# A two-layer MLP in a streaming encoder: seven products in the second layer too, with input sums made in the first

## The chip, the core and the metric

The kernel runs on one NeuronCore of one Trainium2 chip. The metric is the device time of one execution in microseconds. Five engines work side by side, each through its own list of instructions in a fixed order: TensorE (PE, with its weight loads shown as PEld), VectorE (DVE), ScalarE (ACT), GpSimd (POOL) and SyncE (SP), which here issues all DMAs. Semaphores join them.

## The reference

One layer of a hybrid encoder: a token mixer and then an MLP with squared ReLU, on 512 tokens of width 2048 with a hidden width of 8192. All arithmetic is in float32. What matters here is the second sub-layer:

```python
h = x * (1.0 + sc2) + sh2
ff = jnp.square(jax.nn.relu(h @ w_ff1[l])) @ w_ff2[l]
x = layer_norm(ALPHA * x + g2 * ff, ln2_g[l], ln2_b[l])
```

`sc2`, `sh2` and `g2` come from `c @ w_ada + b_ada`, a product of one row with six matrices of 2048 x 2048. `x` is the output of the first sub-layer, `layer_norm(ALPHA * x + g1 * mix)`. `h @ w_ff1` and the product with `w_ff2` are 512 x 2048 x 8192 each.

## The kernel before, in words

A float32 operand is cut into a rounded high part and the rest (`split`, L114: ScalarE writes the high part by L57, VectorE the rest by L60), and every product is made as three matmuls: high x high, high x low, low x high (`mm3`, `mm3s`, `mm3n`, L188 to L204). Weights come from DRAM in loads of 1 MB into four buffers named `raw` (`load`, L118), and their splits go into three buffers each of `wh` and `wl`.

The order of each engine's instructions is set when the program is built: a scheduler takes what is ready in its own model of time, first by place in the program less an offset that `PRIO` (L25) gives to named groups. On the chip that order is fixed; an instruction that waits holds all those behind it on its engine.

*First MLP layer.* `acts` holds the layer's input, transposed and split. The hidden width is done in 16 units of 512. Unit 0 is a plain product. Units 1 to 15 (`ff1_unit`, L1086) use Winograd's form of Strassen's scheme: weights and input are each seen as 2 x 2 blocks, and seven products of half-sized blocks replace eight. The sums of the input (`t3`, `n2`, `n1`, `t4`, L1054 to L1084) are made once. The sums of the weights are made in each unit: eight additions on VectorE. A product is 48 matmuls of 256 columns in two halves of the inner dimension (`c`), each with a split of 128 x 1024. PSUM keeps three running banks: they are read out between accumulations, since some partial sums are used twice. The order of products is a11, s3, s2, a12, s1, a22, s4, and the second one needs three sums of weights. Each quarter of the result (two blocks of 128 features x 256 tokens) goes through ReLU and square on ScalarE and is stored to `h_d` in DRAM (L1145).

*Second MLP layer.* The 8192 hidden features are done in 8 parts of 1024 (`for e in range(NE)`). `hidden` (L1181) loads a part from `h_d` and splits it. `ff2` (L1214) does a block of 512 output features for it: two weight loads, 8 steps of 128 features, 4 token tiles, three matmuls of 512 columns, so 96 a block and 384 a part, in four banks. `ff2_done` (L1193) adds the banks to `ffa` on VectorE (part 0: ScalarE copies).

*Background work.* `bg` holds generators, and `tick` advances the first by one step. `w_quads` (L165) advances it by `pump[0]` steps per weight load. In the second layer these are two `ada_block` jobs, 8 steps each, that make the gate row `g2`; a step loads 1 MB and does two accumulations of 128 x 1024 on VectorE (L63). `pump[0]` is 1, so they lie in parts 0 and 1. Ahead of part 3 (`EB`) the sum so far is multiplied with `g2`, and `ALPHA` times the normalised residual, read back from `xn_d`, is added: 16 tiles of 128 x 512, four VectorE operations each. From part 3 on each bank takes two operations (multiply by `g2`, add).

The last part ends tile by tile with the layer norm statistics and the output.

Of the kernel before, what the change touches and what calls it, by code (L numbers as in the profile page):

```python
# [25 lines left out]
            wo=5000, ln1=150, ff1=3000, ff2=4000, tx=2000, ln2=150, index=-100, topk=60, rope=600, ssm0=600, ssm=300, glu=150,  # L26
# [25 lines left out]
def trunk_kernel(ctx, tc, A, out):  # L52
    nc = tc.nc
# [21 lines left out]
    pools = {n: ctx.enter_context(tc.tile_pool(name="ps_" + n, bufs=b, space=PSUM))  # L75
# [9 lines left out]
    def bank(n="mm"):  # L85
        return pools[n].tile([128, 512], F32, name=n)

# [888 lines left out]
    h_d = dram.tile([16, 128, 4, SEQ], F32, name="h_d")  # L976
# [66 lines left out]
    with prio("ff1"):  # L1043
        for m in range(4):
            r = ev_tile()
            act(r, banks[m], AF.Relu)
            act(r, r, AF.Square)
            nc.sync.dma_start(h_d[0][:, m], r)
# [37 lines left out]
    def ff1_unit(b):  # L1086
        lo, hi, s1, s2 = [None] * 2, [None] * 2, [None] * 2, [None] * 2
# [6 lines left out]
        ca, cb = slice(0, 256), slice(256, 512)  # L1094

        def form(name, c):
            a11, a21, a12, a22 = lo[c][:, :, ca], lo[c][:, :, cb], hi[c][:, :, ca], hi[c][:, :, cb]
            if name == "a11":
                return a11
            if name == "s3":  # L1100
                s1[c], s2[c] = st_tile(), st_tile()
                tt(s1[c], a21, a22, OP.add)
                tt(s2[c], s1[c], a11, OP.add)
                tt(a11, a11, a21, OP.add)
                return a11
            if name == "s2":
                return s2[c]
            if name == "a12":
                return a12
            if name == "s1":  # L1110
                return s1[c]
            if name == "a22":
                return a22
            tt(s2[c], s2[c], a12, OP.add)
            return s2[c]

        def product(ps, name, x, start, stop):
            for c in range(2):
                h = stage.tile([128, 4, 256], F32R, name="wh", bufs=3)
                l = stage.tile([128, 4, 256], F32R, name="wl", bufs=3)  # L1120
                with prio("w_split"):
                    split(h, l, form(name, c))
                for k in range(4):
                    for m in range(2):
                        w = slice(m * 128, m * 128 + 128)
                        mm3s(ps[:, m * 256:m * 256 + 256], h[:, k, w], l[:, k, w], x[:, 4 * c + k, 0],
                            x[:, 4 * c + k, 1], start and (c, k, m) == (0, 0, 0), stop and (c, k, m) == (1, 3, 1))

        def copy(ps):
            o = ev_tile()  # L1130
            with prio("ff1"):
                act(o, ps)
            return o

        def done(o, ps, m0, j, neg):

            with prio("ff1"):
                if o is None:
                    o = ev_tile()
                    act(o, ps, AF.Relu)  # L1140
                else:
                    tt(o, ps, o, OP.add)
                    act(o, o, AF.Relu, scale=-1.0 if neg else 1.0)
                act(o, o, AF.Square)
                nc.sync.dma_start(h_d[b][:, m0:m0 + 2, (lo_t, hi_t)[j]], o.rearrange("p (m n) -> p m n", m=2))  # L1145

        x, z, v = bank(), bank(), bank("sa")
        product(x, "a11", b11, True, False)
        e1 = copy(x)
        product(z, "s3", t3, True, False)  # L1150
        e3 = copy(z)
        product(x, "s2", n2, False, False)
        e2 = copy(x)
        product(v, "a12", b21, True, True)
        done(e1, v, 0, 0, False)
        product(x, "s1", n1, False, False)
        done(e3, x, 2, 1, True)
        product(z, "a22", t4, False, True)
        done(e2, z, 2, 0, True)
        product(x, "s4", b22, False, True)  # L1160
        done(None, x, 0, 1, False)

    for b in range(1, 16):
        ff1_unit(b)
    ph1.close()
    actp.close()

# [3 lines left out]
    NE, EB = 8, 3  # L1171
    HX = ctx.enter_context(tc.tile_pool(name="hx", bufs=1, reuse_waits="tile"))
    FF = ctx.enter_context(tc.tile_pool(name="ff", bufs=1, reuse_waits="tile"))
    ffa = FF.tile([128, NT, D], F32, name="ffa")
    g2 = FF.tile([128, D], F32, name="g2")
    AZ[0] = FF
    bg.extend(ada_block(6 + j, to_rows(lambda i, j=j: g2[:, (2 * j + i) * 512:(2 * j + i + 1) * 512]), True)
              for j in range(2))
    pump[0] = 1

    def hidden(e):  # L1181

        out = []
        for i in range(2):
            r = load(h_d[2 * e + i], [128, 4, 512])
            o = (TX if e == 0 else HX).tile([128, 4, 2, SEQ], F32R, name="tx", bufs=3)
# [4 lines left out]
        return out  # L1191

    def ff2_done(e, nb, t, ps):  # L1193
        cs_ = slice(nb * 512, (nb + 1) * 512)
        with prio("ff2"):
            o = ffa[:, t, cs_]
            if e == 0:
                act(o, ps)
            elif e < EB:
                tt(o, ps, o, OP.add)  # L1200
            else:
# [3 lines left out]
                if e == NE - 1:  # L1205
                    V.bn_stats(out=stats[:, t, nb], in_=o)
# [7 lines left out]
    def ff2(e, nb, h1):  # L1214
        banks = banks4()
# [6 lines left out]
    for e in range(NE):  # L1222
        h1 = hidden(e)
        if e == EB:
            while bg:
                tick()

            for nb in range(4):
                cs_ = slice(nb * 512, (nb + 1) * 512)
                g_ = FF.tile([128, 512], F32, name="lng")  # L1230
                b_ = FF.tile([128, 512], F32, name="lnb")
                nc.sync.dma_start(g_, A["ln1g"][0:1, cs_].to_broadcast([128, 512]))
                nc.sync.dma_start(b_, A["ln1b"][0:1, cs_].to_broadcast([128, 512]))
                ts(g_, g_, ALPHA, None, OP.mult)
                ts(b_, b_, ALPHA, None, OP.mult)
                for t in range(NT):
                    y = FF.tile([128, 512], F32, name="y", bufs=2)
                    nc.sync.dma_start(y, xn_d[t][:, cs_])
                    tt(y, y, g_, OP.mult)
                    tt(y, y, b_, OP.add)  # L1240
                    o = ffa[:, t, cs_]
                    tt(o, o, g2[:, cs_], OP.mult)
                    tt(o, o, y, OP.add)
        if e < NE - 1:
            for nb in range(4):
                ff2(e, nb, h1)
        if e == 0:
            txp.close()
# [118 lines left out]
```

## Time and profile before

| | |
|---|---|
| median of 3 runs | 2313.34 us (2308.38 to 2313.43) |
| the profiled execution | 2313.1 us |
| its span, first to last instruction | 2311.3 us |
| mean granted TensorE clock | 0.988 |
| read from HBM, written | 351.46 MB, 37.75 MB |

A window row of the profile gives a stretch of the span, its length, then for each engine the busy time and, in brackets, the number of instructions that were recorded (some matmuls are missing from a trace), then the granted TensorE clock, the DMA engines' busy share and GB/s. A timeline row gives start, duration, engine, source line, operation, output and inputs, and in brackets the idle time before it with what ended it. A group row gives source line, engine, operation, output and inputs, shape and count; then total busy time and the mean in ns; then the engine's idle time before such instructions and what ended it. Lines such as L57 and L60 are helpers, so groups are told apart by their tiles: `wh` and `wl` are split weights, `raw` a loaded one, `st` a sum of weights, `ev` a piece of hidden output, `adaz` the accumulator of a gate row.

### The profile page before, as it was taken

How to read it: one execution, taken by the hardware profiler on the slowest of the kernel's cores; microseconds unless marked ns; L12 is line 12 of the kernel's file. 1: busy time of each engine (PE TensorE's matmuls, PEld its weight loads, DVE VectorE, ACT ScalarE, POOL GpSimd, SP SyncE). 2: the span in 40 equal slices, each digit the busy share in tenths (PEclk: the TensorE clock that was granted, in tenths of full speed). 3: DMA queues.
4: the chain of work that ended last, by engine and by line, in shares of the span. 5: the costliest groups of instructions: out<-in, count | busy, mean ns of one | idle time of the engine just before them, and what ended most of it. 6: DMA issues, size and time to landing. Idle time of an engine off the chain costs nothing.

```text
span 2311.3 us, 30437 instructions
## 1 busy us (share of the span) xinstructions
PE 2224.7 (96%) x12283; PEld 1910.5 (83%) x12283; DVE 1636.8 (71%) x2300; ACT 967.1 (42%) x1400; POOL 15.7 (1%) x31
## 2 busy tenths in 40 slices
PE   6999999998889999989999999999999999999997
PEld 5778887766667888889999999999888888888886
DVE  7896899998766876676777677676454865545567
ACT  3323434547865214545555555554322222222232
POOL 0000000000000000000000000000000000000000
PEclk9999999999999999999999999999999999999999
DMA  8877562354233776733333333345664543233341
GB/s 313 314 303 266 181 237 92 125 192 144 82 107 111 293 287 233 239 128 108 139 119 142 133 138 137 117 147 206 224 218 146 171 157 128 110 123 133 110 146 73
DMA packets 114053, 391.18 MB, mean 169 GB/s; under 512 B 13428, under 2 KB 49652, under 8 KB 77176
## 3 DMA queue, kind: packets, MB, share of 16 engines
q1 hardware_dynamic: 113912, 389.24, 46.7%
q8 instruction: 96, 1.57, 0.3%
q14 instruction: 45, 0.37, 0.0%
HBM read 351.46 MB, written 37.75 MB: 168 GB/s over the span
## 4 chain that ended last, share of the span: by engine, by line
PE 80%; DVE 12%; ACT 4%; DMA 2%; issue 2%; SPq 0%; DVEq 0%; ACTq 0%
PE mm L202 9%; PE mm L204 9%; PE mm L203 9%; PE mm L197 7%; PE mm L196 7%; PE mm L198 7%; PE mm L191 4%; PE mm L192 4%; PE mm L190 4%; PE sa L204 2%; PE sa L202 2%; PE sa L203 2%; DVE wl L60 2%; ACT uc L57 2%; PE sa L197 1%
## 5 line engine op out<-in xcount | busy, mean ns | idle before, releaser
L57 ACT ACTIVATE wh<-raw 128x1024 fp32r<-128x1024 f32 x302 | 319.6, 1059 | 740.3 <-PE mm L204 519.7
L60 DVE TENSOR_TENSOR wl<-raw,wh 128x1024 fp32r<-128x1024 f32 x302 | 368.5, 1221 | 281.7 <-ACT wh L57 281.0
L63 DVE SCALAR_TENSOR_TENSOR adaz<-raw,cols,adaz 128x1024 f32<-128x1024 f32 (+2 forms) x212 | 239.4, 1138 | 26.3 <-DMA raw<-in_adaR_dram 20.0
L202 PE MATMUL mm<-wh,tx 128*128 128x512 f32 x600 | 234.6, 391 | 1.4 <-DVE ffa L60 1.4
L204 PE MATMUL mm<-wh,tx 128*128 128x512 f32 x600 | 234.1, 390 | 0.0
L203 PE MATMUL mm<-wl,tx 128*128 128x512 f32 x600 | 234.1, 390 | 0.0
L190 PE MATMUL mm<-acts,wh 128*128 128x512 f32 (+1 forms) x568 | 222.9, 396 | 7.2 <-ACT ve L57 3.8
L191 PE MATMUL mm<-acts,wl 128*128 128x512 f32 (+1 forms) x568 | 225.4, 397 | 1.2 <-DVE wl L60 0.9
L192 PE MATMUL mm<-acts,wh 128*128 128x512 f32 (+1 forms) x568 | 223.0, 393 | 0.0
L196 PE MATMUL mm<-tx,wh 128*128 128x256 f32 x720 | 203.5, 283 | 6.1 <-ACT wh L57 6.1
L197 PE MATMUL mm<-tx,wl 128*128 128x256 f32 x720 | 205.3, 285 | 0.9 <-DVE wl L60 0.9
L198 PE MATMUL mm<-tx,wh 128*128 128x256 f32 x720 | 204.6, 284 | 0.0
L197 PE MATMUL mm<-acts,wl 128*128 128x256 f32 x720 | 203.7, 283 | 0.0
L198 PE MATMUL mm<-acts,wh 128*128 128x256 f32 x720 | 203.7, 283 | 0.0
L196 PE MATMUL mm<-acts,wh 128*128 128x256 f32 x720 | 203.7, 283 | 0.0
L203 PE MATMUL mm<-wl,acts 128*128 128x512 f32 x448 | 175.2, 391 | 1.2 <-DVE wl L60 1.0
L204 PE MATMUL mm<-wh,acts 128*128 128x512 f32 x448 | 174.9, 391 | 0.0
L202 PE MATMUL mm<-wh,acts 128*128 128x512 f32 x448 | 174.2, 392 | 0.3 <-DVE z_t L60 0.2
L60 DVE TENSOR_TENSOR wl<-st,wh 128x1024 fp32r<-128x1024 f32 x90 | 110.2, 1225 | 88.9 <-ACT wh L57 88.9
L57 ACT ACTIVATE wh<-st 128x1024 fp32r<-128x1024 f32 x90 | 95.2, 1059 | 126.0 <-PE mm L198 107.4
L196 PEld LDWEIGHTS mm<-tx,wh 128*128 128x128 f32 x720 | 138.3, 192 | 6.7 <-ACT wh L57 6.7
L196 PEld LDWEIGHTS mm<-acts,wh 128*128 128x128 f32 x720 | 138.2, 192 | 0.0
(314 smaller groups left out, 4632.2 us busy)
## 6 DMA issues: line engine op xcount, KB each, us to landing
raw<-in_wff_dram SPq DMA_DIRECT2D x113, 1024.0 KB, 5.0
raw<-in_adaR_dram SPq DMA_DIRECT2D x64, 1024.0 KB, 4.9
raw<-in_adaS_dram SPq DMA_DIRECT2D x32, 1024.0 KB, 9.3
raw<-in_wo_dram SPq DMA_DIRECT2D x16, 1024.0 KB, 6.8
h_d<-ev SPq DMA_DIRECT2D x64, 256.0 KB, 3.8
raw<-h_d SPq DMA_DIRECT2D x16, 1024.0 KB, 4.8
rawx<-in_wff_dram SPq DMA_DIRECT2D x15, 1024.0 KB, 5.4
raw<-in_wconv_dram SPq DMA_DIRECT2D x12, 1024.0 KB, 5.5
```

Source lines behind the costliest of these rows:

```text
L57: S.activation(o, i, f, **kw)
L60: V.tensor_tensor(o, a, b, op=op)
L63: V.scalar_tensor_tensor(o, a, s, b, op0=op0, op1=op1)
L190: T.matmul(ps, wh, xh, start=start, stop=False)
L191: T.matmul(ps, wl, xh, start=False, stop=False)
L192: T.matmul(ps, wh, xl, start=False, stop=stop)
L196: T.matmul(ps, wh, xh, start=start, stop=False, skip_group_check=True)
L197: T.matmul(ps, wl, xh, start=False, stop=False, skip_group_check=True)
L198: T.matmul(ps, wh, xl, start=False, stop=stop, skip_group_check=True)
L202: T.matmul(ps, xh, wh, start=start, stop=False)
L203: T.matmul(ps, xh, wl, start=False, stop=False)
L204: T.matmul(ps, xl, wh, start=False, stop=stop)
```

## The change

1. The seven products become a generator, `strassen`, that both layers use. The order is now a11, a12, s2, a11 + a21 (with t3), s1, a22, s4: the second product needs no sum of weights. All four weight loads of a first-layer unit use the four `raw` buffers (the extra `rawx` buffer goes).
2. In the first layer, units 0 to 11 no longer store plain hidden output. For each unit the three quarters b11, b21, b22 and the four combinations n1, t3, n2, t4 are split into high and low part and stored to `hc_d`, 512 KB each, through two buffers `hc` (`put`, `sums_done`). That is 11 more VectorE operations of 128 x 512 and 7 more on ScalarE a unit. Units 12 to 15 store to `h_d` as before.
3. In the second layer, parts 0 to 5 are done in two half parts each (`ff2_unit`), over two blocks of 512 output features and both halves of tokens and inner dimension. A product is 24 matmuls of 512 columns into a pair of banks; a read is one operation on 128 x 1024. The seven split sums of a part are loaded ready-made from `hc_d`, 1 MB each, into eight buffers `hin`; the next part's are issued product by product in the second half part. The first two sums of part 0 have a place of their own, so they needn't wait for `acts`.
4. Parts 6 and 7 stay plain. PSUM is re-made between the layers as four pairs of banks. The gate row and the residual now lie in part 6 and at the start of part 7: `pump[0]` is 3, and the residual's tiles are steps of the background too (`merge`).

The diff, cut to its core:

```diff
@@ first layer, output
+    QUARTERS = ((0, 0), (1, 1), (1, 0), (0, 1))
+    ORDER = ("b11", "b21", "n2", "t3", "n1", "t4", "b22")
+    def put(b, name, o):
+        e, c = divmod(b, 2)
+        w = ST.tile([128, 2, 2, 256], F32R, name="hc", bufs=2)
+        with prio("hc"):
+            split(w[:, 0], w[:, 1], quad2(o))
+            nc.sync.dma_start(hc_d[e, ORDER.index(name), :, c], w.bitcast(F32))
+    def quarter_done(b, i, j, o):
+        if b < 2 * NS:
+            if (i, j) != (0, 1):
+                put(b, f"b{i + 1}{j + 1}", o)
+        else:
+            with prio("ff1"):
+                nc.sync.dma_start(h_d[b - 2 * NS][:, 2 * i:2 * i + 2, 256 * j:256 * j + 256], quad2(o))
+    def sums_done(b, o):
...
+        sub(b11, b11, b12)
+        put(b, "n1", b11)
+        sub(b12, b22, b12)
+        put(b, "t3", b12)
+        sub(b22, b11, b22, True)
+        put(b, "n2", b22)
+        sub(b21, b22, b21, True)
+        put(b, "t4", b21)
@@ the seven products, for both layers
+        def product(ps, name, x, start, stop):
+            for c in range(2):
+                h = stage.tile(widths, F32R, name="wh", bufs=3)
+                l = stage.tile(widths, F32R, name="wl", bufs=3)
+                with prio("w_split"):
+                    split(h, l, w4[c][name])
+                operate(ps, h, l, x, c, start and c == 0, stop and c == 1)
+        x, z, v = yield
+        product(x, "a11", "b11", True, False)
+        form("s1", "a21", "a22")
+        form("s2", "s1", "a11")
+        read("p1", x)
+        product(v, "a12", "b21", True, True)
+        for c in range(2):
+            with prio("w_split"):
+                tt(w4[c]["a11"], w4[c]["a11"], w4[c]["a21"], OP.add)
+        read("p2", v)
+        product(x, "s2", "n2", False, False)
+        for c in range(2):
+            with prio("w_split"):
+                tt(w4[c]["s2"], w4[c]["s2"], w4[c]["a12"], OP.add)
+        read("p6", x)
+        product(z, "a11", "t3", True, False)
+        read("p7", z)
+        product(x, "s1", "n1", False, False)
+        read("p5", x)
+        product(z, "a22", "t4", False, True)
+        read("p4", z)
+        product(x, "s2", "b22", False, True)
+        read("p3", x)
@@ first layer, loads of a unit
-            if c == 0:
-                hi[c] = load(A["wff1"][b][2], [128, 4, 512])
-            else:
-                hi[c] = load(A["wff1"][b][3], [128, 4, 512], ST, "rawx", 1)
+            hi[c] = load(A["wff1"][b][2 + c], [128, 4, 512])
@@ second layer
+    def sums(e, p):
+        first_two = e == 0 and p < 2
+        r = (HE if first_two else HC).tile([128, 2, 2, 2, 256], F32R, name="hin", bufs=2 if first_two else 8)
+        with prio("hc_load"):
+            nc.sync.dma_start(r.bitcast(F32), hc_d[e, p])
+        return r
+    def ff2_unit(e, cp, h_in, h_next):
...
+        def operate(ps, h, l, name, c, start, stop):
+            p = ORDER.index(name)
+            if c == 0 and h_next is not None:
+                h_next.append(sums(e + 1, p))
+            x = h_in[p]
+            for k in range(2):
+                for t in range(2):
+                    tk = slice(t * 128, t * 128 + 128)
+                    xh, xl = x[:, c, 0, k, tk], x[:, c, 1, k, tk]
...
+                    T.matmul(ps[:, t], xh, h[:, k], start=first, stop=False, skip_group_check=True)
+                    T.matmul(ps[:, t], xh, l[:, k], start=False, stop=False, skip_group_check=True)
+                    T.matmul(ps[:, t], xl, h[:, k], start=False, stop=last, skip_group_check=True)
...
+                if e == 0 and (i, j) not in touched:
+                    act(o, ps, scale=-1.0 if neg else 1.0)
+                    touched.add((i, j))
+                elif neg:
+                    tt(o, o, ps, OP.subtract)
+                else:
+                    tt(o, ps, o, OP.add)
+    for e in range(NS):
+        h_next = [] if e + 1 < NS else None
+        ff2_unit(e, 0, h_in, None)
+        ff2_unit(e, 1, h_in, h_next)
...
+        h_in = h_next
@@ gate row and residual, parts 6 and 7
-    pump[0] = 1
+    bg.extend([g2_job(1), merge(2), merge(3), g2_job(0), merge(0), merge(1)])
+    pump[0] = 3
```

More of the change, by code (lines that the diff above doesn't have):

```diff
@@ L1084, in trunk_kernel, with strassen, form, new_s @@
             parts(t4, a)
+    def strassen(halves, tile4, widths, operate, read):
+        w4 = [dict(zip(("a11", "a21", "a12", "a22"), h)) for h in halves]
+        def form(name, x, y, new=True):
+            for c in range(2):
+                with prio("w_split"):
+                    tt(new_s(c, name) if new else w4[c][name], w4[c][x], w4[c][y], OP.add)
+        def new_s(c, name):
+            w4[c][name] = tile4()
+            return w4[c][name]
+        def product(ps, name, x, start, stop):
[16 more added lines that the diff above has]
+        product(x, "s2", "n2", False, False)
+        for c in range(2):
+            with prio("w_split"):
+                tt(w4[c]["s2"], w4[c]["s2"], w4[c]["a12"], OP.add)
[8 more added lines that the diff above has]
+        read("p3", x)
@@ L1117, in product @@
[L1117 to L1135, printed above, removed]
+            hi[c] = load(A["wff1"][b][2 + c], [128, 4, 512])
+        halves = [(lo[c][:, :, 0:256], lo[c][:, :, 256:512], hi[c][:, :, 0:256], hi[c][:, :, 256:512])
+                  for c in range(2)]
+        inputs = dict(b11=b11, b21=b21, n2=n2, t3=t3, n1=n1, t4=t4, b22=b22)
+        def operate(ps, h, l, name, c, start, stop):
+            x = inputs[name]
+            for k in range(4):
+                for m in range(2):
+                    w = slice(m * 128, m * 128 + 128)
+                    mm3s(ps[:, m * 256:m * 256 + 256], h[:, k, w], l[:, k, w], x[:, 4 * c + k, 0],
+                         x[:, 4 * c + k, 1], start and (k, m) == (0, 0), stop and (k, m) == (3, 1))
@@ L1137, in done, with copy @@
+        part = {}
+        def copy(name, ps):
+            part[name] = ev_tile()
+            act(part[name], ps)
+        def done(i, j, o, ps, neg=False):
             with prio("ff1"):
@@ L1144, in done, with read @@
                 act(o, o, AF.Square)
[L1145 to L1161, printed above, removed]
+            part[i, j] = o
+            quarter_done(b, i, j, o)
+        def read(name, ps):
+            if name in ("p1", "p6", "p7"):
+                with prio("ff1"):
+                    copy(name, ps)
+            elif name == "p2":
+                done(0, 0, part["p1"], ps)
+            elif name == "p5":
+                done(1, 1, part["p7"], ps, True)
+            elif name == "p4":
+                done(1, 0, part["p6"], ps, True)
+            else:
+                done(0, 1, None, ps)
+                sums_done(b, [part[q] for q in QUARTERS])
+        run(strassen(halves, st_tile, [128, 4, 256], operate, read), (bank(), bank(), bank("sa")))
     for b in range(1, 16):
@@ L1204, in ff2_done @@
                 tt(o, o, y, OP.add)
[L1205 to L1206 removed]
+            if e == NE - 1:
+                V.bn_stats(out=stats[:, t, nb], in_=o)
     def ff2_part(h1, ps, t, w):
@@ L1214, in ff2 @@
     def ff2(e, nb, h1):
-        banks = banks4()
+        p2 = [two_banks() for _ in range(2)]
+        banks = [p2[t // 2][:, t % 2] for t in range(NT)]
         for w in w_quads(A["wff2"][e][nb], range(2)):
```

160 lines of the change are left out of this document (99 added, 61 removed).

## The prediction

> **What bounds the kernel now.** I read the page first, then the busy time by stage, then single stretches of the timelines.
>
> ```profile
> span 2311.3 us, 30437 instructions
> PE 2224.7 (96%) x12283; PEld 1910.5 (83%) x12283; DVE 1636.8 (71%) x2300; ACT 967.1 (42%) x1400; POOL 15.7 (1%) x31
> PE 80%; DVE 12%; ACT 4%; DMA 2%; issue 2%; SPq 0%; DVEq 0%; ACTq 0%
> ```
>
> TensorE carries 96% of the span and 80% of the chain that ended last. The profiled execution took 2313.1 us, 1.8 more than its span and 0.2 under the median 2313.34, so the sum below is made against 2313.1 and is also the forecast of the median. By stage (the first MLP layer's start, its 14 full units, then parts of the second layer):
>
> ```profile
> core 0: us, PE busy (x) PEld busy (x) DVE busy (x) ACT busy (x) POOL busy (x), PEclk, DMA share, GB/s
> 986.50:1027.00 40.50, 37.65 (x282) 37.02 (x283) 28.74 (x26) 18.64 (x22) 0.00 (x0) 0.92 0.33 117
> 1027.00:1591.90 564.90, 564.90 (x4711) 564.90 (x4710) 397.73 (x352) 298.90 (x355) 0.95 (x1) 1.00 0.37 133
> 1675.00:1758.00 83.00, 83.00 (x362) 67.66 (x361) 47.96 (x45) 21.30 (x23) 0.95 (x1) 1.00 0.56 203
> 1758.00:1841.00 83.00, 82.34 (x359) 66.97 (x358) 51.21 (x68) 20.84 (x21) 0.00 (x0) 1.00 0.47 163
> 1841.00:1924.00 83.00, 82.26 (x362) 67.99 (x363) 55.66 (x74) 19.84 (x19) 0.00 (x0) 1.00 0.42 141
> ```
>
> From 1027 on TensorE hardly stops (0.66 and 0.74 us in the last two windows) and runs at full clock; VectorE is at 70% in the first layer and 58 to 67% in these windows of the second. What decides there is the number of matmuls and their spacing:
>
> ```profile
> 1154.79 0.28 PE L196 MATMUL mm<-tx,wh 128*128 128x256 f32 x1
> ...
> 1158.38 0.28 PE L196 MATMUL mm<-tx,wh 128*128 128x256 f32 x1
> ...
> 1949.73 0.39 PE L203 MATMUL sa<-wl,tx 128*128 128x512 f32 x1
> ...
> 1955.85 0.39 PE L203 MATMUL sb<-wl,tx 128*128 128x512 f32 x1
> ```
>
> The first pair is 30 matmuls apart: 3.59/30 = 0.1197 us at 256 columns. The second is 27 apart: 6.12/27 = 0.2267 us at 512.
>
> **The change, part by part.**
>
> *Matmuls of the second layer.* A part is 4 blocks x 8 k x 4 t x 3 = 384 matmuls of 512 columns. By seven products it is 2 half parts x 7 x 24 = 336, of the same form. Six parts drop 288: 288 x 0.2267 = **-65.3 us**, if TensorE stays the bound. A half part then lasts 168 x 0.2267 = 38.1 us. The first layer keeps its 336 matmuls a unit (40.2 us).
>
> *What VectorE gets.* Prices:
>
> ```profile
> 1183.03 1.23 DVE L60 TENSOR_TENSOR st<-raw,rawx 128x1024 f32<-128x1024 f32 x1 [0.18 <-DMA rawx<-in_wff_dram]
> 1184.17 0.68 DVE L60 TENSOR_TENSOR ev<-mm,ev 128x512 f32<-128x512 f32 x1
> 1184.77 1.22 DVE L60 TENSOR_TENSOR wl<-raw,wh 128x1024 fp32r<-128x1024 f32 x1
> 1185.91 1.22 DVE L60 TENSOR_TENSOR st<-st,raw 128x1024 f32<-128x1024 f32 x1
> L60 DVE TENSOR_TENSOR y<-mm,g 128x512 f32<-128x512 f32 x53 | 35.5, 686 | 22.6 <-PE mm L204 22.6
> L60 DVE TENSOR_TENSOR ffa<-ffa,y 128x512 f32<-128x512 f32 x96 | 62.7, 684 | 0.3
> L57 ACT ACTIVATE ev<-ev 128x512 f32<-128x512 f32 x109 | 68.6, 631 | 15.8 <-DVE ev L60 13.6
> ```
>
> In a full queue 1024 elements cost 1.14 us from start to start (1.23 alone) and 512 cost 0.60 (0.68 alone); reading PSUM costs the same as SBUF (686 against 684 ns). A half part gives VectorE 14 splits, 8 weight sums and 7 reads of two banks, all of 1024: 29 x 1.14 = 33.1 to 29 x 1.23 = 35.7 us in 38.1, 87 to 94%. A first-layer unit has 397.73/14 = 28.4 us now and gets 4 subtractions and 7 splits of 512: 11 x 0.60 to 0.68 = 6.6 to 7.5, so 35.0 to 35.9 in 40.2, 87 to 89%, in 12 of 16 units (the last four keep their plain output). ScalarE's 298.90/14 = 21.4 us gets 7 x 0.63 = 4.4: no bound. So TensorE remains the longest engine in both layers, but with little air. What such air costs, the earlier stages show:
>
> ```profile
> 80.00:120.00 40.00, 39.67 (x181) 31.99 (x180) 36.05 (x43) 13.31 (x19) 0.00 (x0) 1.00 0.73 275
> 120.00:160.00 40.00, 39.20 (x179) 31.66 (x178) 35.33 (x44) 12.46 (x15) 0.00 (x0) 1.00 0.82 318
> 320.00:360.00 40.00, 39.62 (x174) 31.32 (x173) 39.03 (x68) 16.13 (x25) 0.00 (x0) 1.00 0.69 262
> 360.00:400.00 40.00, 39.64 (x176) 31.33 (x175) 39.60 (x87) 17.04 (x27) 0.00 (x0) 1.00 0.25 90
> 780.00:800.00 20.00, 19.31 (x82) 15.02 (x81) 17.80 (x21) 3.21 (x4) 0.00 (x0) 1.00 0.63 232
> 800.00:820.00 20.00, 20.00 (x90) 16.57 (x89) 16.25 (x14) 5.20 (x5) 0.00 (x0) 1.00 0.98 365
> ```
>
> In the four windows of 40 us VectorE was 88 to 99% busy and TensorE lost 0.33 + 0.80 + 0.38 + 0.36 = 1.87 of 160 us, 1.2%. Over 12 units and 12 half parts (482 + 457 = 939 us) that is **+11 us**; bounds 0 (as now) and, by the window at 780 (0.69 of 20), 3.45% or 32. I take the four, being longer and nearer in load.
>
> *DMA.* A first-layer unit reads 4.19 MB and now writes 3.67 in place of 1.05: 7.86/40.2 = 195 GB/s. The second half of a part reads 4.19 of weights and the next part's sums, 7.34: 11.5/38.1 = 303 GB/s, the first half 110. The window at 800 moved 365 with TensorE full, so **0**, with the stall at each part's border as a rival. Each sum has a whole half part between its load and its use. The weight buffers are again four in all, and a later unit's first two loads wait only for the fourth product's splits.
>
> *Gate row and residual, moved from parts 0 to 3 into parts 6 and 7.* Part 6 now issues three background steps for each of its 8 weight loads: 8 loads of 1 MB, 8 residual steps, 8 loads.
>
> ```profile
> L63 DVE SCALAR_TENSOR_TENSOR adaz<-raw,cols,adaz 128x1024 f32<-128x1024 f32 x169 | 216.6, 1282 | 25.9 <-DMA raw<-in_adaR_dram 20.0 <-DMA adaz<-in_bR_dram 2.9 <-DMA raw<-in_adaS_dram 0.7
> raw<-in_wff_dram SPq DMA_DIRECT2D x113, 1024.0 KB, 5.0
> h_d<-ev SPq DMA_DIRECT2D x64, 256.0 KB, 3.8
> ```
>
> VectorE in part 6: 24 splits 27.4, 32 accumulations at 1.14 to 1.28 (36.5 to 41), 8 residual tiles of 4 x 0.60 (19.2) with their scalings (about 1, an estimate from the 512 price), 24 evacuation operations of 0.60 (14.4): 98 to 103 us against 384 x 0.2267 = 87 of TensorE. Part 7 has 16 splits, the other 8 residual tiles, 32 evacuation operations and 16 statistics: 18.2 + 19.2 + 19.2 + 9.6 = 66, so it can take the rest, and two sets of banks let evacuation lag by a block (21.8 us). Four loads in 10.9 us are 4.19/10.9 = 385 GB/s, over the 365: 11.5 us each, +0.6 in 16/3 groups, 3 us. Bounds 0 and 16 (all of VectorE's excess); I take **+4**, near the DMA's price, since most of the excess can slide. The two windows in which this work now lies lose 0.66 + 0.74: **-1.4**.
>
> *The seam.* New PSUM pairs replace the old banks; the first pair holds the last unit's two accumulators, so its first matmul waits for a 0.6 us ScalarE read and two handovers; sums three to seven can load only after the last product. Bounds 0 and 5 (one 1 MB landing): **+2**.
>
> *Start of the first layer.*
>
> ```profile
> PE mm L196 <- ACT wh L57: 6.1, 3, 4.1
> ```
>
> That wait falls in the window from 986.5, where product two needs three sums of weights. Its new product two needs none and takes input that is ready: up to -6 (2.85 idle and the clock's 8% of 40.5). Against it stand unit 0's sums, 11 x 0.60 = 6.6 us on the busy VectorE. I take **-1**.
>
> Sum: 2313.1 - 65.3 + 11 + 4 - 1.4 + 2 - 1 = 2262.4, forecast **2262**.
>
> **Rivals.**
>
> *B: VectorE binds in order.* A late operation in its queue holds the splits behind it. For it: 94% if each operation costs 1.23. Against: a split can be done some 3 us early (three weight buffers, two of 2.7 us ahead, less 2.4 for both engines). At the 3.45% of the window at 780 the losses are 32 in place of 11: 2283; with part 6's whole 16, 2295.
>
> *C: stalls that cool TensorE.* In the window from 986.5 a wait of 4.1 us went with a clock of 0.92, 3.2 us more. If late sums or weights stop it so at each of the five borders between parts and at the seam, 6 x 7.3 = 44 us: 2306. [...] Against C: 303 GB/s is under what the trace has moved without a stall.
>
> *D: slower, by the stores of sums.* The split that makes a sum ready needs one of two store buffers, and at a unit's end four come in a row. ScalarE's next one then stands until a store has landed (3.8 us for 256 KB, here 512), and the next unit's weight splits stand behind it. With about 3 us of air, a stand of 8.5 us a unit turns to 5.5 lost, x 12 = 66: 2328. It decides from 4.3 us a unit on (51/12). Against it: these steps have the lowest priority of the stage and fill gaps, and late in a unit few loads are in flight.
>
> **How the numbers follow.** Forecast 0.62, B 0.15, C 0.07, D 0.11, between forecast and no change by some mixture 0.05. Low end 2249: no loss in either layer (-11) and 2 off elsewhere. High end 2303: B whole, and most of C. That leaves out D, part of C and the mixture, under 2 in 10. What a measurement of this kernel can tell from no change is about 0.3%, 7 us: under 2306.4 faster. Faster 0.84 (forecast, B, most of C), same 0.05, slower 0.11.
>
> **What would show it.** Right: 336 matmuls spaced 0.2267 in a part, about 76 to 78 us from part to part; first-layer units of 40.2 to 41; VectorE at 85 to 95% in both; part 6 at 88 to 95 us; clock 1.00. Wrong: matmuls waiting for weight splits in most half parts (B), a clock under 0.95 at the borders (C), ScalarE standing for stores of sums in the first layer (D). If parts stay at 85 us or units pass 44, the forecast fails.

## The result, and the profile after

The changed kernel takes 2273.88 us (median of 4 runs, 2271.86 to 2276.16), the kernel before 2313.39 (4 runs, 2308.38 to 2314.33): a ratio of 0.9834 with a 95% interval of 0.9816 to 0.9851. It is faster by 39.5 us; the forecast was 51, its range 2249 to 2303. The profiled execution took 2272.77 us, so the sum of 2262.4 is short by 10.4.

First the page after: span, busy engines, and the engines' shares of the chain that ended last.

```profile
span 2270.6 us, 30412 instructions
PE 2161.3 (95%) x11995; PEld 1853.9 (82%) x11995; DVE 1867.0 (82%) x2516; ACT 1055.8 (46%) x1528; POOL 15.7 (1%) x31
PE 57%; DVE 25%; DMA 10%; ACT 5%; issue 2%; SPq 0%; DVEq 0%; ACTq 0%
```

The recorded matmuls fell by 288, as counted. But TensorE's share of the chain fell from 80% to 57%: VectorE and DMA now set the pace in some places. The windows say in which: start of the first layer, its units with sums (up to the end of the first plain unit), the last three plain units, second layer's first part, two later parts, then two stretches of parts 6 and 7.

```profile
986.50:1027.00 40.50, 39.71 (x329) 39.30 (x328) 35.70 (x38) 24.03 (x31) 0.00 (x0) 1.00 0.50 174
1027.00:1480.00 453.00, 437.91 (x3598) 432.81 (x3598) 363.24 (x387) 259.41 (x343) 0.00 (x0) 1.00 0.56 194
1480.00:1604.00 124.00, 123.43 (x1027) 123.03 (x1026) 85.52 (x77) 64.28 (x78) 0.00 (x0) 1.00 0.42 151
1606.50:1683.00 76.50, 74.12 (x321) 60.35 (x322) 60.55 (x56) 34.73 (x34) 0.00 (x0) 1.00 0.72 270
1683.00:1759.00 76.00, 76.00 (x337) 62.92 (x337) 66.01 (x58) 30.66 (x29) 0.00 (x0) 1.00 0.54 207
1835.00:1911.00 76.00, 76.00 (x337) 62.97 (x336) 66.93 (x59) 29.76 (x28) 0.00 (x0) 1.00 0.54 207
2063.00:2150.00 87.00, 78.52 (x332) 62.62 (x331) 81.11 (x88) 17.93 (x19) 0.95 (x1) 0.96 0.80 294
2150.00:2258.00 108.00, 107.27 (x464) 86.77 (x463) 99.59 (x152) 31.94 (x38) 0.00 (x0) 1.00 0.46 161
```

The first number after the length is TensorE's busy time. In the second layer's steady parts TensorE never stands still, with VectorE at 66.93 of 76 (88%). In the first layer's units with sums it stands idle for 15.1 of 453 us, with VectorE at 80%. So the idle time isn't where VectorE is fullest. In the kernel before, the same stretch had no idle time at all:

```profile
1027.00:1480.00 453.00, 453.00 (x3779) 453.00 (x3777) 319.39 (x283) 237.08 (x283) 0.00 (x0) 1.00 0.37 133
```

Idle time is less than the time lost. The profile models a matmul's end: it puts it 0.28 us after the start, though the next one starts after 0.12, and the first one behind a stall takes longer (0.22 at the stall shown below). By the matmuls done in the stretch, 3598 in place of 3779, 181 x 0.1199 = 21.7 us were lost. So idle times are used below to compare runs, and starts of matmuls to add up.

By the starts of the matmuls in both traces, the first layer (from its first unit with seven products to its last matmul) went from 615.4 to 628.6 us, +13.2; the seam to the second layer from 0.1 to 1.9, +1.8; the second layer from 706.6 to 651.8, -54.8; what lies ahead and behind, -0.9. Together -40.7, the difference of the spans.

The +13.2 is the sum of two larger numbers. Unit 1, the first with seven products, took 41.7 us in place of 51.2; units 2 to 15 took 586.9 in place of 564.2, and those of them with sums (2 to 11) 42.3 each on average in place of 40.3. The gain of unit 1, before and after:

```profile
976.00:1027.00 51.00, 44.07 (x333) 43.12 (x333) 39.17 (x36) 25.20 (x33) 0.00 (x0) 0.93 0.36 124
976.00:1027.00 51.00, 50.21 (x414) 49.80 (x415) 46.13 (x47) 32.06 (x45) 0.00 (x0) 1.00 0.40 138
```

The waits of 1027 to 1480 in the changed kernel (who waited, for whom; total, times, longest):

```profile
ACT hc L57 <- DMA hc_d<-hc: 111.5, 58, 5.2
DVE st L60 <- DMA raw<-in_wff_dram: 62.5, 22, 4.5
PEld mm L203 <- DVE wl L60: 18.8, 23, 1.5
PE mm L203 <- DVE wl L60: 14.0, 21, 1.3
```

ScalarE stands 111.5 us for the store buffers `hc`, 10.5 a unit. VectorE stands 62.5 us in forms of weight sums (`st`) whose 1 MB load hasn't landed. TensorE stands for low parts of weights (`wl`). One of these stalls, on VectorE, ScalarE and TensorE:

```profile
1220.74 1.23 DVE L60 TENSOR_TENSOR wl<-st,wh 128x1024 fp32r<-128x1024 f32 x1 [1.18 <-ACT wh L57]
1224.60 1.22 DVE L60 TENSOR_TENSOR st<-raw 128x1024 f32<-128x1024 f32 x1 [2.64 <-DMA raw<-in_wff_dram]
1225.74 1.22 DVE L60 TENSOR_TENSOR st<-st,raw 128x1024 f32<-128x1024 f32 x1
1226.88 1.22 DVE L60 TENSOR_TENSOR wl<-raw,wh 128x1024 fp32r<-128x1024 f32 x1
```

```profile
1213.68 0.63 ACT L57 ACTIVATE hc<-ev 128x512 fp32r<-128x512 f32 x1 [2.34 <-DMA hc_d<-hc]
...
1225.78 0.63 ACT L57 ACTIVATE hc<-ev 128x512 fp32r<-128x512 f32 x1 [3.40 <-DMA hc_d<-hc]
```

```profile
1228.15 0.39 PE L203 MATMUL mm<-acts,wl 128*128 128x256 f32 x1 [1.00 <-DVE wl L60]
```

Read backwards: TensorE waits for the `wl` of 1226.88, which lies in VectorE's fixed order behind two forms, the first of which waited 2.64 us for a load. The trace shows that load issued at 1217.85, as soon as a split on VectorE had freed a `raw` buffer; that split lay behind ScalarE's, which had stood for a store at 1213.68. About one stall of 0.8 to 1.3 us comes in a unit; with the shorter ones there are 25 in the stretch. Loads and stores of the stretch, before and after (KB each, median us to landing):

```profile
raw<-in_wff_dram SPq DMA_DIRECT2D x35, 1024.0 KB, 5.5
```

```profile
raw<-in_wff_dram SPq DMA_DIRECT2D x44, 1024.0 KB, 6.4
hc_d<-hc SPq DMA_DIRECT2D x77, 512.0 KB, 7.2
```

The second loss is one stall in part 6, the longest of TensorE's waits behind 1027, at 2089. Below it stands the second half's spread, and then part 6 as a whole, by its own bounds:

```profile
2098.03 3.34 PE L244 MATMUL two<-adaz,ones 128*128 128x512 f32 x4 [8.48 <-DVE adaz L63]
...
2167.59 1.88 PE L244 MATMUL two<-adaz,ones 128*128 128x512 f32 x4
```

```profile
2067.30:2168.90 101.60, 93.12 (x393) 74.04 (x392) 93.99 (x105) 24.99 (x26) 0.95 (x1) 0.97 0.84 306
```

These four matmuls spread half of the finished gate row over all partitions. They stand in TensorE's fixed order at a place that VectorE's accumulations (`adaz`) reached late. Behind the stall the four took 3.34 us, where the second half's took 1.88.

### The profile page after: what moved, and what is told of

Same layout as the page of the kernel before. It is cut to its first block, busy times and chain, and to the rows that moved or that the text cites. A ratio compares the mean times of both kernels' runs of the same rounds, so it can differ in the third digit from the quotient of the medians.

```text
span 2270.6 us, 30412 instructions
## 1 busy us (share of the span) xinstructions
PE 2161.3 (95%) x11995; PEld 1853.9 (82%) x11995; DVE 1867.0 (82%) x2516; ACT 1055.8 (46%) x1528; POOL 15.7 (1%) x31
## 4 chain that ended last, share of the span: by engine, by line
PE 57%; DVE 25%; DMA 10%; ACT 5%; issue 2%; SPq 0%; DVEq 0%; ACTq 0%
DVE wl L60 7%; PE two L1296 7%; PE two L1297 7%; PE two L1295 7%; DMA raw<-in_wff_dram 6%; PE mm L197 4%; PE mm L198 4%; PE mm L196 4%; DVE st L60 3%; PE mm L210 3%; PE mm L208 3%; PE mm L209 3%; DMA hc_d<-hc 2%; PE mm L203 2%; PE mm L204 2%
## 5 line engine op out<-in xcount | busy, mean ns | idle before, releaser
L57 ACT ACTIVATE wh<-raw 128x1024 fp32r<-128x1024 f32 x332 | 349.6, 1057 | 468.1 <-PE two L1297 146.6
L60 DVE TENSOR_TENSOR wl<-raw,wh 128x1024 fp32r<-128x1024 f32 x332 | 403.9, 1221 | 68.1 <-ACT wh L57 67.1
L1295 PE MATMUL two<-wh,hin 128*128 128x512 f32 x672 | 262.2, 390 | 2.6 <-ACT ev L57 1.6
L1296 PE MATMUL two<-wl,hin 128*128 128x512 f32 x672 | 262.1, 390 | 1.4 <-DVE wl L60 1.4
L1297 PE MATMUL two<-wh,hin 128*128 128x512 f32 x672 | 262.0, 390 | 0.0
L63 DVE SCALAR_TENSOR_TENSOR adaz<-raw,cols,adaz 128x1024 f32<-128x1024 f32 (+2 forms) x212 | 239.2, 1138 | 19.5 <-DMA raw<-in_adaR_dram 15.3
L203 PEld LDWEIGHTS mm<-acts,wl 128*128 128x128 f32 x720 | 138.0, 192 | 19.8 <-DVE wl L60 19.8
L1295 PEld LDWEIGHTS two<-wh,hin 128*128 128x128 f32 x672 | 126.2, 188 | 29.4 <-ACT ev L57 1.8
L1296 PEld LDWEIGHTS two<-wl,hin 128*128 128x128 f32 x672 | 126.2, 188 | 27.9 <-DVE wl L60 1.7
L1297 PEld LDWEIGHTS two<-wh,hin 128*128 128x128 f32 x672 | 126.2, 188 | 26.5
```

The costliest lines, as they stand in the source:

```text
L57: S.activation(o, i, f, **kw)
L60: V.tensor_tensor(o, a, b, op=op)
L203: T.matmul(ps, wl, xh, start=False, stop=False, skip_group_check=True)
L1295: T.matmul(ps[:, t], xh, h[:, k], start=first, stop=False, skip_group_check=True)
L1296: T.matmul(ps[:, t], xh, l[:, k], start=False, stop=False, skip_group_check=True)
L1297: T.matmul(ps[:, t], xl, h[:, k], start=False, stop=last, skip_group_check=True)
```

## The experiments

The theories that the expectations name: *W*, the new order of products with four `raw` buffers lets weights come late by itself; *V*, VectorE has too much to do; *S*, ScalarE stands for the two store buffers; *T*, the stores' traffic; *Q*, the order of SyncE's queue, where loads and stores wait behind each other. "Idle" is TensorE's, of the 453 us from 1027. "First layer" runs from the start of unit 1 to its last matmul, "second layer" from its first to its last matmul. Runs without an interval are single runs; beside each stands the kernel before on the same chip.

| run | us | before | idle | ScalarE for `hc` stores | VectorE for loads | load to landing | first layer | second layer |
|---|---|---|---|---|---|---|---|---|
| changed kernel | 2273.88 | 2313.39 | 15.1 | 111.5 | 62.5 | 6.4 | 628.6 | 651.8 |
| no sums | 2252.60 | 2315.18 | 1.1 | 9.1 | 12.3 | 5.5 | 607.8 | 653.6 |
| no stores | 2256.36 | 2315.18 | 0.8 | 7.2 | 10.3 | 4.9 | 606.8 | 653.2 |
| forms later | 2280.94 | 2315.18 | 15.3 | 108.6 | 60.2 | 6.4 | 629.0 | 657.9 |
| traffic only | 2262.93 | 2310.11 | 1.8 | 7.5 | 22.6 | 5.0 | 612.8 | 656.2 |
| stores by GpSimd | 2316.02 | 2310.11 | 36.5 | 91.9 | 33.9 | 7.4 | 668.0 | 656.4 |
| one `hc` buffer | 2365.96 | 2312.39 | 72.3 | 54.2 | 27.1 | 5.1 | 722.4 | 652.7 |
| five `ev`, two `hc` | 2293.57 | 2312.44 | 18.2 | 119.2 | 66.7 | 6.1 | 636.9 | 665.9 |
| five `ev`, three `hc` | 2291.01 | 2312.39 | 17.2 | 42.6 | 71.1 | 6.5 | 635.5 | 666.4 |
| the same, stores by GpSimd, row moved | 2304.95 | 2312.44 | 23.2 | 66.3 | 38.4 | 7.8 | 650.8 | 656.9 |

**No sums.** Units 2 to 11 store plain quarters, as before; the second layer reads the sums of units 0 and 1.

```diff
-        if b < 2 * NS:
+        if b < 2:
...
-            nc.sync.dma_start(r.bitcast(F32), hc_d[e, p])
+            nc.sync.dma_start(r.bitcast(F32), hc_d[0, p])
```

> Leaves out the sums: units 2 to 11 of the first layer store their four plain quarters (as before the change), and all parts of the second layer read the sums of units 0 and 1. New product order and four weight buffers stay. Measured on TensorE's idle time from 1027 to 1480 us, 15.1 in the changed kernel and 0 before. Theory W (late weight loads: the fourth buffer is freed by the sixth product, and the sums s1, s2 that come right after product one wait for its next load while the splits stand behind them in VectorE's queue): if order and buffers alone make it, 10 to 15 us stay. Theory S (ScalarE standing for the two store buffers) and theory V (VectorE 89% loaded): under 2 us stay. The whole then takes 2256 to 2262 by S or V, about 2270 by W.

Measured: 2252.60 us, idle 1.05.

```profile
1027.00:1480.00 453.00, 451.95 (x3765) 451.54 (x3764) 320.46 (x292) 234.90 (x287) 0.00 (x0) 1.00 0.39 140
```

Without the sums the new order of products and the four buffers cost 1 us of idle time here, and the first layer is 20.8 us shorter than the changed kernel's. W by itself falls.

**No stores.** The sums are formed and split; only the stores of units 2 to 11 are left out.

```diff
-            nc.sync.dma_start(hc_d[e, ORDER.index(name), :, c], w.bitcast(F32))
+            if b < 2:
+                nc.sync.dma_start(hc_d[e, ORDER.index(name), :, c], w.bitcast(F32))
```

> Leaves out the DMA stores of the sums of units 2 to 11; the sums are still formed and split, and the second layer reads the sums of units 0 and 1 throughout. S: ScalarE no longer stands for a store buffer (111 us of such waits go), and TensorE's 15.1 us idle from 1027 to 1480 falls under 3. V: it stays at 12 to 15, the load on VectorE is the same. W: weight loads land in about 5 us in place of 6.7, so it falls by a third to two thirds, to 5 to 10.

Measured: 2256.36 us.

```profile
1027.00:1480.00 453.00, 452.25 (x3769) 452.04 (x3769) 386.82 (x406) 272.12 (x358) 0.00 (x0) 1.00 0.32 116
```

VectorE has all its work, 386.82 us (85%), and TensorE stands for 0.75. The first layer is 21.8 us shorter. V falls: the loss hangs on the stores.

**Forms later.** The two forms behind product one go behind product two.

```diff
-        form("s1", "a21", "a22")
-        form("s2", "s1", "a11")
         product(v, "a12", "b21", True, True)
+        form("s1", "a21", "a22")
+        form("s2", "s1", "a11")
```

> The whole computation; the four weight sums s1 and s2 are put behind product two in place of behind product one, in both layers, so they come two half products (5.8 us) later in VectorE's order. W: VectorE's waits for weight loads (62 us in 22) mostly go and TensorE's idle time from 1027 to 1480 falls from 15.1 to under 6. S and V: it stays at 13 to 17, since loads on both engines and the stores are the same. In the second layer's parts all theories expect no change (76.0 us each).

Measured: 2280.94 us, idle 15.3, VectorE's stand for loads 60.2. Moving the form that waits changed nothing in the first layer. The second layer took 657.9 us, little above the 651.8 to 656.4 of the six kernels that leave its order as it is.

**Row later.** For the stall in part 6: the first spread three steps later, 3.5 steps a load.

```diff
-    bg.extend([g2_job(1), merge(2), merge(3), g2_job(0), merge(0), merge(1)])
-    pump[0] = 3
+    bg.extend([g2_job(1, 3), merge(2), merge(3), g2_job(0, 0), merge(0), merge(1)])
+    pump[0] = 3.5
```

> The whole computation; in part 6 the two matmuls that spread the gate row's first half are put three background steps (one weight load) later, with 3.5 steps a load in place of 3. The changed kernel's TensorE stood 8.6 us there for VectorE's accumulations. If it is a matter of place in TensorE's queue: the 8.6 us go, 2264 to 2267 in all. If part 6 is short of DMA or VectorE throughput (rival): the stall moves to the weight splits and 5 to 9 us of idle time stay in parts 6 and 7, 2269 to 2273.

Measured: 2292.34 us. TensorE's waits from 2063 to 2258:

```profile
PE two L244 <- DVE y L60: 22.6, 2, 22.3
PE two L209 <- DVE wl L60: 1.9, 1, 1.9
```

The wait for `adaz` is gone, so its place in the order was the cause. But the second spread, now at the end of part 6, stood 22.3 us, as the rest had been drained in a burst ahead of it.

**Stores by GpSimd.** SyncE's queue then holds no store in the first layer.

```diff
-            nc.sync.dma_start(hc_d[e, ORDER.index(name), :, c], w.bitcast(F32))
+            nc.gpsimd.dma_start(hc_d[e, ORDER.index(name), :, c], w.bitcast(F32))
```

> The whole computation; the stores of the sums are issued by GpSimd in place of SyncE, so they no longer stand in the same queue as the weight loads, and no weight load stands behind a store that waits for its split. The traffic and the two store buffers stay. TensorE's idle time from 1027 to 1480 us was 15.1 in the changed kernel. Theory Q (queue: loads and stores hold each other up in SyncE's order and in one DMA queue): stores land sooner than the 7.2 us, ScalarE's 111 us of standing for store buffers shrinks, and the idle time falls under 5. Theory S (two buffers are too few whatever the queue): ScalarE still stands over 60 us and idle time stays over 8. Theory T (the traffic itself makes weight loads land late): the landing of weight loads stays at 6 to 7 us and 10 to 15 us of idle time stay.

Measured: 2316.02 us, idle 36.5. Issues in the stretch, then waits:

```profile
raw<-in_wff_dram SPq DMA_DIRECT2D x40, 1024.0 KB, 7.4
hc_d<-hc POOLq DMA_DIRECT2D x73, 512.0 KB, 3.8
```

```profile
ACT hc L57 <- DMA hc_d<-hc: 91.9, 28, 6.8
DVE hc L60 <- ACT hc L57: 65.1, 21, 6.7
DVE st L60 <- DMA raw<-in_wff_dram: 33.9, 11, 5.0
```

The median store landed in 3.8 in place of 7.2 us, the stand for loads was halved, and TensorE lost more. The scheduler set the splits in other places: ScalarE's stands were fewer and longer, and VectorE, which makes the low half of a split, now stood behind them. The loads took 7.4 us, 1.0 more than in the changed kernel, although no store was in their queue. Q alone falls.

**Traffic only.** As many bytes are stored to the same places, but out of the resident `t3` (units 2 to 11, so the second layer computes with other data): no store waits for a split, no split for a store.

```diff
-            nc.sync.dma_start(hc_d[e, ORDER.index(name), :, c], w.bitcast(F32))
+            nc.sync.dma_start(hc_d[e, ORDER.index(name), :, c], (w if b < 2 else t3[:, 0:2]).bitcast(F32))
```

> From unit 2 on the stores of the sums take their bytes from a finished tile (t3) in place of the store buffer, so they carry the same traffic, but no store buffer waits for its landing and no store for its split; the sums that the second layer reads are not the right ones. S: TensorE's idle time from 1027 to 1480 falls under 3 us, as with the stores left out (0.75). T: it stays at 10 to 15, with weight loads landing in 6 to 7 us and VectorE standing some 60 us for them. Q lies between: loads can still stand behind stores in the one DMA queue, 3 to 8.

Measured: 2262.93 us, idle 1.8. With nothing to wait for, the scheduler put all these stores between 960 and 1149. A window from there, and the issues in it:

```profile
1060.00:1148.00 88.00, 87.68 (x731) 87.48 (x730) 76.17 (x81) 54.70 (x73) 0.00 (x0) 1.00 0.91 339
```

```profile
hc_d<-tx SPq DMA_DIRECT2D x38, 512.0 KB, 10.2
raw<-in_wff_dram SPq DMA_DIRECT2D x8, 1024.0 KB, 5.9
```

At 339 GB/s, where the changed kernel has 186 and TensorE stands for 2.8 us, TensorE stood for 0.3. Only unit 1, which lies in the first part of that burst, took 45.7 us, 4.0 more than in the changed kernel. In the steady units traffic alone doesn't do it: the stores have to be tied to the splits.

**Row spread.** The row's halves and their merges in the other order, each spread three steps later, and the rest runs on in part 7's first half.

```diff
+        for _ in range(3):
+            yield
...
-    bg.extend([g2_job(1), merge(2), merge(3), g2_job(0), merge(0), merge(1)])
+    bg.extend([g2_job(0), merge(0), merge(1), g2_job(1), merge(2), merge(3)])
...
-            while bg:
-                tick()
```

> The whole computation; the two gate row jobs and the residual change places (first blocks 0 and 1), the matmuls that spread each half of the row come three steps after its last accumulation, and what is left runs on through the first half of part 7 in place of being issued in one go at its start. In the changed kernel TensorE stood 8.65 us for the first of these matmuls. If that stall is a matter of place: it goes, no stall of over 3 us comes in parts 6 and 7, and the time is 2263 to 2267. If part 6 is bound by VectorE or DMA (rival): 4 to 9 us of idle time appear at weight splits or at the second spread, 2268 to 2273.

Measured: 2271.10 us, a single run, not told apart from the changed kernel's 2271.86 to 2276.16. Its first layer stood for 13.6 us of the 453, much as before the edit; its second layer took 645.9 us, 5.9 less. The whole doesn't show this: what comes behind the last matmul took 1.8 us more, and unit 1 began 4.2 us later (its start lies between 972.6 and 980.2 in the runs here). Stretches of parts 6 and 7:

```profile
2066.00:2150.00 84.00, 83.31 (x358) 66.89 (x357) 75.38 (x79) 22.79 (x23) 0.95 (x1) 1.00 0.81 298
2150.00:2258.00 108.00, 102.95 (x437) 82.72 (x435) 99.58 (x154) 26.86 (x33) 0.00 (x0) 0.98 0.45 161
```

In part 6 TensorE stood for 0.7 in place of 8.5 us; 2.4 us came back as a wait in part 7, before its end (at 2258 this run had already finished its matmuls for 3 us).

**One buffer, three buffers, both cures.** A test of S: one `hc` buffer, then three. For three, one of the six `ev` buffers was given up and two small tiles, `ident` and `stats`, got shorter lives.

```diff
-        return ST.tile([128, 512], F32, name="ev", bufs=6)
+        return ST.tile([128, 512], F32, name="ev", bufs=5)
...
-        w = ST.tile([128, 2, 2, 256], F32R, name="hc", bufs=2)
+        w = ST.tile([128, 2, 2, 256], F32R, name="hc", bufs=3)
```

> The whole computation; one store buffer (hc) in place of two, which makes the suspected wait worse and leaves the work and the traffic as they are. S: the seven splits of a unit come one landing apart, ScalarE and VectorE stand far longer, and TensorE's idle time from 1027 to 1480 rises from 15.1 us to over 40; the whole is over 2295. If the buffers do not matter: 13 to 17, and 2270 to 2276.

> The whole computation; three store buffers (hc) in place of two. The space comes from one of the six buffers of hidden pieces (ev) and from giving the identity and the statistics shorter lives. S: a burst of four sums then stands for one landing in place of two; ScalarE's standing for store buffers from 1027 to 1480 falls from 111 us to under 60, and TensorE's idle time there from 15.1 us to 3 to 8. If two buffers are not what counts (rival: the place of these splits in ScalarE's order, made for landings shorter than the real 7.2 us), the scheduler puts them earlier with three buffers and the idle time stays at 10 to 16.

> The whole computation, with three store buffers and the gate row's spread put later. If both stalls are matters of buffers and of place, their gains add: 8.65 less about 3 us from the row, and 5 to 12 us from the first layer, so 2257 to 2268 against 2273.9. If three buffers do not help: 2269 to 2273.

Measured: 2365.96 us with one, 2291.01 with three, and 2287.53 (ratio 0.9889, 0.9872 to 0.9906; idle 17.1, second layer 657.8) with three and the row spread. With one buffer ScalarE stood 5.98, 3.70 and 3.46 us in a row for stores, and with it the read-outs that free the accumulators: four stalls of TensorE of about 18 us, 72.0 of the 72.3. With three the stand shrank as expected, the idle time did not:

```profile
ACT wh L57 <- PE mm L207: 85.6, 64, 1.8
...
ACT hc L57 <- DMA hc_d<-hc: 42.6, 21, 4.1
```

```profile
1027.00:1480.00 453.00, 435.77 (x3597) 431.18 (x3596) 361.96 (x385) 258.70 (x344) 0.00 (x0) 1.00 0.55 189
```

**Control, and both cures at once.** The control keeps two `hc` buffers and all the rest of that edit, and adds 512 bytes of padding ahead of the second layer's tiles. The other run has three buffers, the row spread, the padding, and the stores on GpSimd.

```diff
+    pad = FF.tile([128, 128], F32, name="pad")
```

> Control for the run with three store buffers, which gave up one of the six ev buffers and moved two small tiles to find the room: here ev has five, the store buffers stay two, and a tile of 512 bytes that nobody reads puts the second layer's tiles back to the addresses of the changed kernel. In the window 1027 to 1480, TensorE was idle for 15.1 us in the changed kernel and 17.2 with three store buffers and five ev. Theory X (the third store buffer helped and the fifth ev buffer took it back): idle 20 us or more here. Theory Y (the coupling is in SyncE's queue, where weight loads stand behind stores that wait for their splits): idle 14 to 17, as changed. Second layer, by the addresses: matmuls 0.2267 us apart as in the changed kernel, first second-layer matmul to last 650 to 654; if the spacing of 0.2324 that the three-buffer runs showed has another cause, 664 to 668.

> Three store buffers (and five ev), the stores issued from GpSimd's queue so that no weight load stands behind a store, the row's spread matmul three steps later and the row's halves in the other order, and the 512 bytes of padding. Theory Y (the two waits feed each other through SyncE's queue, so that neither cure alone was enough): idle of TensorE in 1027 to 1480 at 6 us or less, and with the second layer at 646 a time of 2255 to 2263. Theory X (five ev buffers): idle 15 to 20 us, time 2268 to 2275. Theory Z (VectorE's order about the loads, whatever the queue): idle 12 us or more with VectorE's waits for loads at 50 us or more, time 2265 to 2275. If the padding does not bring back the spacing of 0.2267 us, each of these times is 14 us longer.

Measured: 2293.57 us for the control; 2304.95 for the other (12 runs, 2296.07 to 2312.27; ratio 0.9963, 0.9950 to 0.9977). The control's waits and windows:

```profile
ACT hc L57 <- DMA hc_d<-hc: 119.2, 62, 5.1
...
ACT wh L57 <- PE mm L207: 28.9, 32, 1.8
```

```profile
1027.00:1480.00 453.00, 434.84 (x3592) 429.41 (x3591) 363.72 (x387) 259.84 (x343) 0.00 (x0) 1.00 0.55 186
1683.00:1759.00 76.00, 76.00 (x329) 61.61 (x328) 64.36 (x56) 29.86 (x29) 0.00 (x0) 1.00 0.54 200
```

Control and three-buffer run differ in the third buffer and the padding alone. ScalarE's stand for stores went from 119.2 to 42.6 us, TensorE's idle time from 18.2 to 17.2, and units 2 to 12 together from 465.8 to 465.1. 56.7 of the 76.6 us came back as ScalarE waiting for TensorE to free a `wh`: it was early now, to no use. So the stand of two buffers, long as it is, is not by itself what stops TensorE; S in that form falls, though one buffer shows that the stand can. X falls too. With one `ev` buffer fewer the idle time rose from 15.1 to 18.2, but units 2 to 12 took 465.0 us before and 465.8 after: the control's matmuls of 256 columns filled a little less of the stretch (3592 took 434.84 us of busy time, the changed kernel's 3598 took 437.91), so more of the same time was idle. Both cures together gave 23.2, so Y falls; VectorE's stand for loads was 38.4, under the 50 that Z wanted, so Z isn't confirmed either.

The padding didn't bring the old spacing back: 329 matmuls in 76 us where the changed kernel has 337. By their starts they are 0.2324 us apart, not 0.2267, in all four kernels with that edit. That is the 14 us by which the control's second layer is longer than the changed kernel's, and the 11 to 12 us by which the two that also spread the row are longer than the run that only spreads it. The padding can't settle whether the place in SBUF is the cause: it lies in the pool `ff`, while `wh` and `wl`, which every matmul here reads, come from the pool `stage`, opened right behind the one that lost the two small tiles.

The control's first layer is 8.2 us longer than the changed kernel's, and 7.6 of them are unit 1 (49.3 us in place of 41.7; 48.4 to 50.8 in all four kernels with that edit). There TensorE waited once for a read-out on ScalarE, which came behind splits of sums:

```profile
1004.68 0.58 PE L205 MATMUL mm<-tx,wh 128*128 128x256 f32 x1 [6.79 <-ACT ev L57]
```

Which part of that edit brings this stall was not tried. So the totals of these four runs carry some 20 us that the number of store buffers doesn't explain, and only units 2 to 12 compare them.

What stands for the first layer: the idle time is there only when stores hang on the splits. Take away the sums, the stores, or that tie, and it is 0.8 to 1.8 us in the stretch. With it there is a ring: store lands, split, weight split behind it on ScalarE and VectorE, `raw` buffer free, load, form, weight split. Widening one link (third buffer) or cutting one (SyncE's queue), or both, changed which wait is longest and didn't shorten the units: with the stores on SyncE, units 2 to 11 took 42.0 to 42.4 us on average with two buffers or three, and 45.8 and 43.6 with the stores on GpSimd. Which link carries it is left open: each edit also moved the scheduler's order, and no run held that order fixed. No version that does the whole work was shown to beat the changed kernel; the row spread alone comes level with it.

## Why the prediction was right, and where its sizes were off

The terms, each against what the starts of the matmuls show:

- *288 matmuls, -65.3.* Right: 288 fewer recorded. A part took 76.2 us, as worked out, in place of 87.2 (parts 3 to 6 before): six times that is -66.0. The spacing of 0.2267 held in parts 1 to 5.
- *Air on VectorE, +11.* This is the mis-sized term. It was spread over both layers by one rule, 1.2% at a VectorE load of 88 to 99%. The second layer's share, 457 us x 1.2% = 5.4, was 0 at 88%. The first layer's share, 482 x 1.2% = 5.6, was 22.8 (units 2 to 15; 15.7 of it shows as idle time, 15.1 and 0.6). The rule came from stages without buffers that wait for a store; the no-stores run at 85% stood for 0.75, so load alone prices nothing here. The bounds, 0 and 32, held both.
- *DMA, 0.* Right for the second layer (207 GB/s with no idle time), and in the steady units traffic alone was harmless at 339. But with the stores the weight loads landed in 6.4 us in place of 5.5, which the sum took as nothing.
- *Part 6 and the row, +4, and -1.4 where they had been.* Part 6 took 101.6 us and part 7 89.4, before 87.2 and 88.1: +15.7, just inside the bounds of 0 and 16. Parts 1 and 2, which had taken 89.0 and 90.2, gave back 4.8 in place of 1.4. The working compared totals of VectorE with totals of TensorE. What failed was the assumption that most of the excess can slide: the spread matmul can't, and one stall of 8.48 us, with the slow matmuls behind it, holds most of it.
- *The seam, +2.* 1.8 us of waiting; the first part lost 0.5 more beside its count of matmuls than before.
- *The start, -1.* Unit 1 took 9.5 us less, more than the bound of -6. The bound counted 2.85 us of idle time in the window from 986.5. But the longest of the three waits, 4.08 us, ends where that window begins, so it was left out.

```profile
986.50 0.39 PE L196 MATMUL mm<-tx,wh 128*128 128x256 f32 x1 [4.08 <-ACT wh L57]
```

The misses: -0.7 (matmuls), +17.2 and -5.4 (air), +11.7 and -3.4 (row), +0.3 (seam and first part), -8.5 (start), and -0.9 ahead of and behind the two layers. They make +10.3; between the spans it is 10.0, and the rest is rounding. So the mechanism that was to bring the gain was right, but that the time came within 12 us of the forecast is partly luck: two losses that had been taken 17.2 and 11.7 us too small stood against a gain taken 8.5 too small, and against two smaller misses of 5.4 and 3.4.

Three of the named signs of being right did not come. Units 2 to 11 took 42.3 us on average in place of 40.2 to 41, and one took 44.2, past the 44 named as failure. VectorE was at 80% in the first layer, under 85. Part 6 took 101.6 us in place of 88 to 95.

The rivals. B, VectorE's order: a late form did hold the splits behind it, in the first layer, at 2.0 us a unit, but because a load was late, not because of VectorE's load; in the second layer it didn't happen. C, stalls that lower the clock: no border between steady parts stalled, so it cost nothing there. It came once, in part 6, where the four matmuls behind the stall took 1.5 us longer than their like. The clock was 1.00 over the first layer's window from 1027, with its stalls of up to 1.3 us, and 0.96 over the window of the 8.48 us stall; how the clock depends on the length of a stall was not shown. D, the store buffers: its place was right, and ScalarE's stand was even longer than assumed, 10.5 us a unit in place of 8.5. Its price was wrong: 2.0 a unit, not 5.5, since most of the stand takes the place of ScalarE's own waiting for a free `wh` (56.7 of 76.6 us, by the control). The one-buffer run, 72 us idle, is what D described.

## What to carry to other kernels

When a change adds stores out of a small ring of buffers to a stage, draw the ring before pricing it: who frees a buffer, what stands behind that engine, and which load waits for that. An average load of an engine priced nothing here: 88% cost 0 in one layer and 80% went with 15 us of idle time in the other. A long stand in the list of waits isn't yet the cause: cut it with one more buffer and look whether the idle time follows. Look for the one instruction of a background job that lies in the bound engine's order, for its place decides, not the job's total. And add up a change from start to start of the same work, unit by unit: idle time showed 15.1 us where 21.7 were lost, and a window that began just behind a wait left out the gain.

## What the runs showed of the hardware

- Stores of 512 KB issued by GpSimd landed in 3.8 us (median), by SyncE in 7.2, while the 1 MB loads beside them went from 6.4 to 7.4. Sooner stores and later loads came together; the order of the splits had changed too, so no run shows that one made the other.
- 339 GB/s ran beside TensorE at 87.68 of 88 us and a clock of 1.00.
- The same matmuls of 512 columns ran 0.2324 us apart in place of 0.2267 in the four kernels in which two small tiles had shorter lives (329 in 76 us in place of 337, at a clock of 1.00, in the windows of the control). 512 bytes of padding, meant to put the second layer's own tiles back to their place in SBUF, didn't change it. That the place of the operands is the cause was not tried by itself.
- Four matmuls of one form took 3.34 us right behind a stall of 8.48 us, and 1.88 us where none came before.
